# GpSimd's four multiplications of y by the last norm's row wait until the last column pair's sevens are folded

## The chip, the core and the metric

The kernel runs on one core of one Trainium2 chip. The metric is the device time of one execution in microseconds (us). The core has five engines that run their own instruction streams side by side: TensorE (PE, matrix products, with its weight loads listed apart as PEld), VectorE (DVE), ScalarE (ACT), GpSimd (POOL) and SyncE (SP, which here issues the DMA transfers). They meet only at semaphores: an instruction waits until another engine or a transfer has counted a semaphore up.

## The reference, cut to what matters

One decoder layer on 256 rows of 2048 columns: a token mixer (two groups of attention heads), then a channel mixer, each with a norm before and after. The change lies in the channel mixer's end, which is

```python
def rmsnorm(x, g):
    y = xf * lax.rsqrt(jnp.mean(xf * xf, axis=-1, keepdims=True) + EPS)
    return (y * g.astype(jnp.float32)).astype(x.dtype)
...
h = rmsnorm(x, pre_ffn_g[l])
u = causal_dwconv(h @ w_up[l], conv_w[l], conv_b[l])
gate, val = jnp.split(u, 2, axis=-1)
y = (jax.nn.gelu(gate, approximate=True) * val) @ w_down[l]
x = x + rmsnorm(y, post_ffn_g[l])
```

w_down has 5632 rows and 2048 columns, in float32. The last line divides y by its root mean square over the 2048 columns, multiplies by the row post_ffn_g and adds x.

## The kernel before

All products run on TensorE in a split form: a float32 weight tile `raw` that a DMA has brought is rounded by ACT into a high part (`whi`, L118 or L287), and DVE subtracts to get the rest (`wlo`, L121 or L288: `wlo = raw - whi`, two inputs in SBUF). A product is then three matmuls: high by high, high by low, low by high. There are five buffers for `raw`, five for `whi`, five for `wlo`. SP issues the load of a unit of 512 KB when DVE's subtraction has freed a `raw` buffer.

The channel mixer's 5632 inner columns are done in two halves of 22 blocks of 128. In each half, first the up-projections fill G (22 tiles of 128 x 512, high and low), then the down-projection adds its products to y, kept in `y_sb` (128 x 2 x 2048: two row blocks t, four column blocks n of 512). The down-projection goes over column pairs, `for n in (0, 2)`. Within a pair, some of the eleven steps u are done by `seven` (a 2 x 2 block product with seven products instead of eight; its four extra sums lie in the PSUM banks a, c, d, f and its combined weight tiles are made by DVE at L998 to L1001) and the rest by `four`, four plain products of the banks. The PSUM banks of seven's extra sums are brought into `y_sb` by `fold`: an ACT copy (L1035) and eight DVE operations, L1036 to L1043, of which the last one writes y22, columns 1536 to 2047 of row block 1, when n is 2.

When a column block is complete, `down` adds its bank to `y_sb` (DVE, L965), squares and sums it on ACT (L967), and, in the second half, multiplies it by the norm's row `gbf` on GpSimd (L969), in place. For the second half's first pair (n = 0, so the columns 0 to 1023 of both row blocks) these four multiplications, 128 x 512 each, are not issued at once: `later_on` collects their arguments in `gains`, and the loop issues them later, in the second pair's step i = 2 (`i == max((0, *at))`, where `at` is (0, 2)), on the lines just behind that pair's `fold`. They stand behind the fold in the program's text only: nothing that they read or write is touched by the fold.

DVE's, ACT's, GpSimd's and SP's order is made by a scheduler from the program's dependencies; TensorE's is the order of the text. At the very end (from L1128) all orders are that of the text. After the loop, TensorE finishes the last column block: for row block 0 with full 512-wide matmuls (L975, bank e), for row block 1 with two halves of 256 columns (L284, banks b1). Some units of that part are kept in `rest`. Then come `rstd_y` (a power on GpSimd, L1093), `finish` (L1104, DVE: y times the root plus x) and the output transfers.

The places that the steps below touch:

- L965, L967, L969: `down`; L1036 to L1043: `fold`; L1064 to L1066: the issue of the four multiplications.
- L121 and L288: DVE's subtraction for a weight unit, for `four` and `seven`. TensorE's matmuls with `wlo` wait for it.
- L1072: ACT's two copies of y (row block 1, columns 1536 to 2047) into the banks b1.
- L89 to L93: `w_parts` places `wlo` within its buffer at an offset of 14 x 4 or 4 x 4 elements, by the unit's turn; L49: `ROOM`, an unused tile of 112 columns in the pool `small`.

Memory is handed out pool by pool, one behind the other: `const`, `main`, `wp`, `small`, and behind `small` the pools `mixp` (with oT), `att`, `hold` and `ffn` (with G), which are opened later.

Of the kernel before, what the change touches and what calls it, by code (L numbers as in the profile page):

```python
# [8 lines left out]
F32 = mybir.dt.float32  # L9
# [3 lines left out]
ALU = mybir.AluOpType  # L13
# [4 lines left out]
P = 128  # L18
# [15 lines left out]
def hybrid_layer(ctx: ExitStack, tc: tile.TileContext, x, pre_mix_g, w_in, b_forget, sinks,  # L34
# [3 lines left out]
    pe, act, dve, pool, sp = nc.tensor, nc.scalar, nc.vector, nc.gpsimd, nc.sync  # L38
# [7 lines left out]
    small = ctx.enter_context(tc.tile_pool(name="small", bufs=4))  # L46
# [5 lines left out]
    def bank(tag="acc"):  # L52
        return ps.tile([P, 512], F32, tag=tag, bufs=4, name="bank_" + tag)
# [236 lines left out]
    with tc.tile_pool(name="mixp", bufs=1) as mp:  # L290
# [311 lines left out]
        for p0, npair, cols in ((0, 3, 384), (3, 3, 384), (6, 2, 272)):  # L602
# [13 lines left out]
            for t, b in enumerate(b2):  # L616
# [5 lines left out]
                if cols == 272:  # L622
                    dve.scalar_tensor_tensor(z[:, t, :], b[:, 256:272], rpre[t], bfb,
                                             op0=ALU.mult, op1=ALU.add)
# [195 lines left out]
    with tc.tile_pool(name="ffn", bufs=1) as fp:  # L820
# [27 lines left out]
        y_sb = main.tile([P, 2, D], F32, tag="y", name="y_sb")  # L848
# [59 lines left out]
        for half in range(2):  # L908
# [52 lines left out]
            gains = []  # L961

            def down(t, n, b, gain=None):
                ys = y_sb[:, t, n * 512:(n + 1) * 512]
                dve.tensor_tensor(ys, b, ys, op=ALU.add)  # L965
                if half:
                    act.activation(junk, ys, AF.Square, scale=D ** -0.5,  # L967
                                   accum_out=ysq[t][:, n:n + 1])
                    (gain or pool.tensor_tensor)(ys, ys, gbf[:, n * 512:(n + 1) * 512], op=ALU.mult)  # L969
# [17 lines left out]
            def seven(n, u, last, banks, opened):  # L987

                b, e, g, a, c, d, f = banks
                k = half * FHALF + u * 2  # L990
                top, low = [w_load(w_rows(w_down, k + i, 1, n * 512, 1024), 1, 1024)[0]
                            for i in range(2)]
                b11, b12, b21, b22 = (x[:, i:i + 512] for x in (top, low) for i in (0, 512))
                s1, s2, s3, s4 = [(sums[:, u, i * P:i * P + P],
                                   sums[:, u, 512 + i * P:640 + i * P]) for i in range(4)]
                (w11,) = split_into(w_parts(UNIT, held=False), top, 1)
                w21, w22 = split_into(w_parts(UNIT, held=False), low, 2)
                dve.tensor_tensor(b11, b12, b11, op=ALU.subtract)  # L998
                dve.tensor_tensor(b12, b22, b12, op=ALU.subtract)
                dve.tensor_tensor(b22, b22, b11, op=ALU.subtract)  # L1000
                dve.tensor_tensor(b21, b21, b22, op=ALU.subtract)  # L1001
                products(a, parts_of(u * 2, 0), *w11, opened, last)
                products(b, parts_of(u * 2 + 1, 0), *w21, opened)
                products(e, s4, *w22, opened)

                def others():
                    t1, t3 = split_into(w_parts(UNIT, held=False), top, 2)
                    t4, t2 = split_into(w_parts(UNIT, held=False), low, 2)
                    products(d, s1, *t1, opened, last)
                    products(f, s3, *t3, opened, last)  # L1010
                    products(c, s2, *t2, opened, last)
                    products(g, parts_of(u * 2 + 1, 1), *t4, opened)

                return others

            def four(n, u, pair, opened):
                hi, lo = w_unit(w_rows(w_down, half * FHALF + u * 2, 2, n * 512, 512), 2, 512)
                for i in range(2):
                    for t in range(2):
                        products(pair[t], parts_of(u * 2 + i, t), hi[:, i, :], lo[:, i, :], opened,  # L1020
                                 u == FHALF // 2 - 1 and i == 1)

            def fold(n, a, c, d, f):

                y11, y12, y21, y22 = (y_sb[:, t, m * 512:(m + 1) * 512] for t in range(2)
                                      for m in (n, n + 1))
                if half == 0:
                    act.copy(y11, a)
                    dve.tensor_tensor(y22, c, y11, op=ALU.add)
                    dve.tensor_tensor(y12, d, y22, op=ALU.add)  # L1030
                    dve.tensor_tensor(y21, f, y22, op=ALU.add)
                    dve.tensor_tensor(y22, d, y21, op=ALU.add)
                else:
                    s = fp.tile([P, 512], F32, tag="s", name="s")
                    act.copy(s, a)  # L1035
                    dve.tensor_tensor(y11, a, y11, op=ALU.add)  # L1036
                    dve.tensor_tensor(s, c, s, op=ALU.add)
                    dve.tensor_tensor(y12, y12, s, op=ALU.add)
                    dve.tensor_tensor(y12, d, y12, op=ALU.add)
                    dve.tensor_tensor(s, f, s, op=ALU.add)  # L1040
                    dve.tensor_tensor(y21, y21, s, op=ALU.add)
                    dve.tensor_tensor(s, d, s, op=ALU.add)
                    dve.tensor_tensor(y22, y22, s, op=ALU.add)  # L1043

            for n in (0, 2):
                opened = []
                tail = half and n
                at = SEVENS[half][n // 2]
                shared = [bank("att") for _ in range(4 if at else 0)]
                b, e, g = [bank() for _ in range(3)]  # L1050
                h = None if tail else bank()
                for i in range(FHALF // 2 - len(at)):
                    others = None
                    if i in at:
                        u = at.index(i)
                        others = seven(n, u, u == len(at) - 1, (b, e, g, *shared), opened)
                    four(n, len(at) + i, (b, g), opened)
                    if not tail:
                        four(n + 1, len(at) + i, (e, h), opened)
                    if others:  # L1060
                        others()
                    if at and i == at[-1]:
                        fold(n, *shared)
                    if i == max((0, *at)):  # L1064
                        for args, kw in gains:
                            pool.tensor_tensor(*args, **kw)  # L1066
                    if tail and i == (at[-1] + 4 if at else 0):
                        b1 = [bank("att"), bank("att")]
                        for x, cs in zip(b1, halves):
                            pe.matmul(x[:, cs], G[0][:, 0:P], G[0][:, 0:256], start=True,  # L1070
                                      stop=False)
                            act.copy(x[:, cs], y_sb[:, 1, 1536:2048][:, cs])  # L1072
                later_on = None if tail else lambda *args, **kw: gains.append((args, kw))
                for t, x in enumerate((b, g)):
                    down(t, n, x, later_on)
                if not tail:
                    for t, x in enumerate((e, h)):
                        down(t, n + 1, x, later_on)
# [30 lines left out]
        for u in range(len(at), FHALF // 2):  # L1109
# [4 lines left out]
            for i in range(2):  # L1114
                k = u * 2 + i
                args = k, hi[:, i, :], lo[:, i, :]
# [61 lines left out]
```

## Time and profile before

| what | value |
|---|---|
| time, median of 3 runs | 1058.31 us (1058.13 to 1058.46) |
| the profiled execution's own time | 1058.56 us |
| its span, first instruction to last | 1056.8 us |
| TensorE busy | 1046.5 us (99%), 5920 matmuls |
| VectorE busy | 820.8 us (78%) |
| ScalarE busy | 635.5 us (60%) |
| GpSimd busy | 259.0 us (25%) |
| granted TensorE clock | 0.998 of full speed |
| DMA, mean over the span | 195 GB/s read from HBM and written |

How to read it: the profile takes one execution, with each instruction's start and duration. The page sums the busy time by engine and by line, and follows the chain of work that ended last back from the end. The views of the trace quoted below give single instructions: start in us from the span's start, duration in us, engine, line, operation, what is written and read, and in brackets how long the engine stood idle before it and for whom. "xN" joins N neighbours of one kind. Matmuls overlap, so a matmul of 512 columns is listed with 0.39 us while the next one starts 0.227 us after it: the spacing of starts is what counts.

### The profile page before, as it was taken

What the parts mean: (1) busy time and instruction counts of PE and PEld (TensorE: products, weight loads), DVE (VectorE), ACT (ScalarE), POOL (GpSimd) and SP (SyncE); (2) the same over time, 40 slices, a digit from 0 to 9 for tenths busy, and PEclk for the clock granted to TensorE, in tenths of its full rate; (3) what the DMA queues carried; (4) which work ended last, traced back from release to release, by engine and by line L of the source; (5) the groups of instructions that cost most, each with busy time, mean ns of one, the idle gap of its engine ahead of it and who ended that gap; (6) DMA issues with size and microseconds to landing.
All of it is one profiled execution on the core that took longest, in us unless ns stands there. A gap on an engine that the chain in (4) does not pass through costs nothing.

```text
span 1056.8 us, 16351 instructions
## 1 busy us (share of the span) xinstructions
PE 1046.5 (99%) x5920; PEld 910.4 (86%) x5920; DVE 820.8 (78%) x1324; ACT 635.5 (60%) x1094; POOL 259.0 (25%) x282
## 2 busy tenths in 40 slices
PE   9999999999999999999999999999999999999996
PEld 7889988888889888888888888888888888888786
DVE  5989877886468787777768888867787777788983
ACT  7777757767557656656555555546566565655560
POOL 4253245431122433311112000003432221200301
PEclk9999999999999999999999999999999999999999
DMA  8645666655875766666665566766656665647483
GB/s 291 194 124 180 181 191 202 175 153 161 298 237 186 220 202 196 201 186 199 193 199 149 188 221 204 235 198 192 187 179 210 192 198 186 192 149 233 156 274 126
DMA packets 161965, 207.09 MB, mean 196 GB/s; under 512 B 6844, under 2 KB 131036, under 8 KB 160860
## 3 DMA queue, kind: packets, MB, share of 16 engines
q1 hardware_dynamic: 161564, 205.65, 62.0%
q8 instruction: 46, 0.75, 0.3%
q10 hardware_dynamic: 320, 0.40, 0.1%
q14 instruction: 35, 0.29, 0.1%
HBM read 201.68 MB, written 4.21 MB: 195 GB/s over the span
## 4 chain that ended last, share of the span: by engine, by line
PE 89%; DVE 4%; DMA 2%; issue 2%; ACT 1%; POOL 0%; SPq 0%; DVEq 0%; POOLq 0%; ACTq 0%
PE bank_acc L262 21%; PE bank_att L262 15%; PE bank_acc L284 13%; PE bank_acc L975 12%; PE bank_acc L269 11%; PE bank_att L269 7%; PE bank_att L975 2%; DMA raw<-in_w_down_dram 2%; DVE wlo L121 1%; PE bank_att L450 1%; PE bank_att L485 1%; PE bank_att L494 1%; DVE wlo L288 1%; PE bank_acc L881 1%; PE bank_acc L225 1%
## 5 line engine op out<-in xcount | busy, mean ns | idle before, releaser
L121 DVE TENSOR_TENSOR wlo<-raw,whi 128x1024 fp32r<-128x1024 f32 (+3 forms) x329 | 400.6, 1231 | 121.5 <-ACT whi L118 114.3
L118 ACT CAST whi<-raw 128x1024 fp32r<-128x1024 f32 (+3 forms) x328 | 333.5, 1033 | 174.6 <-issue 84.5
L262 PE MATMUL bank_acc<-hT,whi 128*128 128x512 f32 x1024 | 245.5, 392 | 0.0
L262 PEld LDWEIGHTS bank_acc<-hT,whi 128*128 128x128 f32 x1024 | 188.2, 188 | 37.1
L857 POOL TENSOR_TENSOR u<-u,rowf 128x256 f32<-128x256 f32 x88 | 95.6, 1107 | 440.1 <-DVE u L856 437.2
L262 PE MATMUL bank_att<-hT,whi 128*128 128x512 f32 x704 | 165.7, 390 | 0.0
L975 PE MATMUL bank_acc<-whi,G 128*128 128x512 f32 x492 | 159.5, 389 | 0.0
L262 PEld LDWEIGHTS bank_att<-hT,whi 128*128 128x128 f32 x704 | 130.6, 188 | 26.2
L269 PEld LDWEIGHTS bank_acc<-hT,wlo 128*128 128x128 f32 x1024 | 123.5, 188 | 3.2
L269 PE MATMUL bank_acc<-hT,wlo 128*128 128x256 f32 x1024 | 125.8, 278 | 0.0
L975 PEld LDWEIGHTS bank_acc<-whi,G 128*128 128x128 f32 x492 | 92.4, 188 | 19.0
L975 PE MATMUL bank_acc<-wlo,G 128*128 128x512 f32 x246 | 95.9, 390 | 0.4 <-DVE wlo L121 0.4
L269 PEld LDWEIGHTS bank_att<-hT,wlo 128*128 128x128 f32 x704 | 83.6, 188 | 1.9
L269 PE MATMUL bank_att<-hT,wlo 128*128 128x256 f32 x704 | 84.0, 277 | 0.0
L284 PE MATMUL bank_acc<-whi,oT 128*128 128x512 f32 (+1 forms) x272 | 81.8, 379 | 0.0
L287 ACT CAST whi<-raw 128x1024 fp32r<-128x1024 f32 (+1 forms) x56 | 51.7, 942 | 35.2 <-PE bank_acc L975 15.9
L288 DVE TENSOR_TENSOR wlo<-raw,whi 128x1024 fp32r<-128x1024 f32 (+1 forms) x56 | 62.2, 1133 | 6.5 <-ACT whi L287 6.5
L284 PEld LDWEIGHTS bank_acc<-whi,oT 128*128 128x128 f32 x272 | 50.2, 188 | 9.3
L975 PEld LDWEIGHTS bank_acc<-wlo,G 128*128 128x128 f32 x246 | 46.2, 188 | 10.2 <-DVE wlo L121 0.8
L284 PE MATMUL bank_acc<-wlo,oT 128*128 128x512 f32 (+1 forms) x136 | 51.2, 377 | 0.0
L859 ACT ACTIVATE yg<-u,cw 128x256 f32<-128x256 f32 x44 | 26.5, 602 | 37.2 <-POOL u L857 37.2
L284 PE MATMUL bank_acc<-whi,hT 128*128 128x384 f32 (+1 forms) x192 | 46.9, 323 | 0.0
(250 smaller groups left out, 1317.7 us busy)
## 6 DMA issues: line engine op xcount, KB each, us to landing
raw<-in_w_up_dram SPq DMA_DIRECT2D x176, 512.0 KB, 4.5
raw<-in_w_down_dram SPq DMA_DIRECT2D x88, 512.0 KB, 4.9
raw<-in_w_in_dram SPq DMA_DIRECT2D x51, 512.0 KB, 5.0
raw<-in_w_out_dram SPq DMA_DIRECT2D x32, 512.0 KB, 4.6
raw<-in_w_in_dram SPq DMA_DIRECT2D x16, 384.0 KB, 3.3
cb<-c_dram SPq DMA_DIRECT2D x8, 256.0 KB, 4.5
x_sb<-in_x_dram SPq DMA_DIRECT2D x2, 1024.0 KB, 6.0
x_dram<-x_sb SPq DMA_DIRECT2D x2, 1024.0 KB, 5.8
```

The costliest lines, as they stand in the source:

```text
L118: i1 = act.copy(hi[:, cs], raw[:, cs])
L121: i2 = dve.tensor_tensor(lo[:, cs], raw[:, cs], hi[:, cs].bitcast(F32), op=ALU.subtract)
L225: pe.matmul(b, hi[:, a, m * P:(m + 1) * P], hT[:, kt, 0:512], start=(kt == 0), stop=(kt == KT - 1))
L262: pe.matmul(b, hi[:, a, m * P:(m + 1) * P], hT[:, kt, 0:512], start=(kt == 0), stop=(last == (0, kt)))
L269: pe.matmul(b[:, 256:512], lo[:, a, m * P:(m + 1) * P], hT[:, u * 4 + a, 0:256], start=False, stop=(last == (1, u * 4 + a)))
L284: pe.matmul(b, a, r[:, cols], start=(first and i == 0), stop=(last and i == 2))
L287: act.copy(hi, src)
L288: dve.tensor_tensor(lo, src, hi.bitcast(F32), op=ALU.subtract)
L450: pe.matmul(sb[e][:, cs], a[r, t * P:(t + 1) * P], b[r, 0:nk], start=(n == 0), stop=(n == 2))
L857: pool.tensor_tensor(u[:, 2:258], u[:, 2:258], rowf, op=ALU.mult)
L859: act.activation(y, u[:, 2:258], AF.Identity, bias=cw[:, 3, ch:ch + 1], scale=cw[:, 2, ch:ch + 1])
L975: pe.matmul(b, x, r, start=b not in opened and not i, stop=closes and i == 2)
```

## The change

```diff
                     if i == max((0, *at)):
+                        if gains:
+                            past = small.tile([P, 1], F32, tag="past", bufs=1, name="past")
+                            tc.keep_in_program_order(
+                                pool.tensor_scalar(past, y_sb[:, 1, 1536:1537], 1.0, None,
+                                                   op0=ALU.mult))
                         for args, kw in gains:
-                            pool.tensor_tensor(*args, **kw)
+                            tc.keep_in_program_order(pool.tensor_tensor(*args, **kw))
```

A small GpSimd operation, `past`, is put ahead of the four multiplications. It reads one column of y22, the block that `fold` writes last (L1043), so it cannot start before the fold has ended; the four are held behind it in GpSimd's order. `past` itself is used by nobody.

GpSimd's stream at this place, as a difference (minus: before, plus: changed; `y_sb` is y, `gbc_ffn` the norm's row, `u` the convolution's input):

```order
 L857 TENSOR_TENSOR u_3946<-u_3946,rowf 128x256
 L857 TENSOR_TENSOR u_3947<-u_3947,rowf 128x256
-L1066 TENSOR_TENSOR y_sb<-y_sb,gbc_ffn 128x512 x4
+L1068 TENSOR_SCALAR past<-y_sb 128x1
+L1071 TENSOR_TENSOR y_sb<-y_sb,gbc_ffn 128x512 x4
 L969 TENSOR_TENSOR y_sb<-y_sb,gbc_ffn 128x512 x3
```

The stream has one instruction more, ahead of the four; the four keep their place between the last convolution's `u` and the last three multiplications. Their time moves, since `past` waits for VectorE.

VectorE's stream at the fold, the same before and in the changed kernel (the instruction that `past` waits for is L1043; `wlo` and `rest` are low parts of weight units):

```order
L121 TENSOR_TENSOR wlo<-raw,whi 128x1024
L1038 TENSOR_TENSOR y_sb<-y_sb,s 128x512
L121 TENSOR_TENSOR wlo<-raw,whi 128x1024
L1039 TENSOR_TENSOR y_sb<-bank_att,y_sb 128x512
L1040 TENSOR_TENSOR s<-bank_att,s 128x512
L121 TENSOR_TENSOR wlo<-raw,whi 128x1024
L1041 TENSOR_TENSOR y_sb<-y_sb,s 128x512
L1042 TENSOR_TENSOR s<-bank_att,s 128x512
L121 TENSOR_TENSOR wlo<-raw,whi 128x1024
L1043 TENSOR_TENSOR y_sb<-y_sb,s 128x512
L121 TENSOR_TENSOR rest<-raw,rest 128x1024
L121 TENSOR_TENSOR wlo<-raw,whi 128x1024
```

No instruction of VectorE, ScalarE, TensorE or SyncE moves. In the built program the tile `past` takes 32 bytes of each partition at the end of the pool `small`, and every tile of the pools behind it, oT and G among them, lies 32 bytes further on than before.

## The prediction

> **What bounds the kernel now.** First the page:
>
> ```profile
> span 1056.8 us, 16351 instructions
> PE 1046.5 (99%) x5920; PEld 910.4 (86%) x5920; DVE 820.8 (78%) x1324; ACT 635.5 (60%) x1094; POOL 259.0 (25%) x282
> PE 89%; DVE 4%; DMA 2%; issue 2%; ACT 1%; POOL 0%; SPq 0%; DVEq 0%; POOLq 0%; ACTq 0%
> ```
>
> TensorE is the bound: it is busy 99% and holds 89% of the chain that ended last. GpSimd is on that chain with 0%. So the four multiplications can only matter through what they do to TensorE's supply. The chain in order of time, at the place where they run (about 987 to 997 us), shows VectorE in it twice:
>
> ```profile
> 993.75 2.32 DVE wlo L121
> ...
> 1004.34 1.22 DVE wlo L288
> ...
> 1006.34 11.56 PE bank_acc L975 x51
> ```
>
> Before and after this stretch the chain is TensorE alone. The timeline of GpSimd and VectorE says why (the third row is the same multiplication form elsewhere, with the minimum, median and maximum in ns):
>
> ```profile
> L1066 POOL TENSOR_TENSOR y_sb<-y_sb,gbc_ffn x4: 2265/2473/2977, 987.2 to 994.9; 128x512 f32<-128x512 f32 x4
> 987.16 10.05 POOL L1066 TENSOR_TENSOR y_sb<-y_sb,gbc_ffn 128x512 f32<-128x512 f32 x4 [53.07 <-ACT junk L967]
> L709 POOL TENSOR_TENSOR mix_sb<-mix_sb,gbc_mix x9: 743/1291/1744, 299.6 to 333.0; 128x512 f32<-128x512 f32 x7, 128x256 f32<-128x256 f32 x2
> ```
>
> ```profile
> 979.70 0.69 DVE L288 TENSOR_TENSOR wlo<-raw,whi 128x512 fp32r<-128x512 f32 x1
> 987.43 1.22 DVE L121 TENSOR_TENSOR wlo<-raw,whi 128x1024 fp32r<-128x1024 f32 x1
> 988.57 1.28 DVE L965 TENSOR_TENSOR y_sb<-bank_acc,y_sb 128x512 f32<-128x512 f32 x2
> ...
> 991.80 2.03 DVE L288 TENSOR_TENSOR wlo<-raw,whi 128x1024 fp32r<-128x1024 f32 x1 [0.21 <-ACT whi L287]
> 993.75 2.31 DVE L121 TENSOR_TENSOR wlo<-raw,whi 128x1024 fp32r<-128x1024 f32 x1
> 995.99 2.91 DVE L288 TENSOR_TENSOR wlo<-raw,whi 128x512 fp32r<-128x512 f32 x2
> ```
>
> A multiplication that takes 1.29 us at the median of L709 takes 2.27 to 2.98 us here. Meanwhile VectorE's subtractions, 1.22 us for 1024 columns and 0.69 us for 512, take 2.03, 2.31 and (a pair, 0.69 + 1.22 less the 0.09 by which neighbours overlap, so 1.82) 2.91 us. They take turns: each multiplication makes one subtraction wait, and VectorE loses 0.81 + 1.09 + 1.09 = **2.99 us**. The two L965 additions, which have one input in PSUM, lose nothing in the same ten microseconds.
>
> **What TensorE loses to that.** TensorE's starts around the two places:
>
> ```profile
> 995.09 0.61 PE L975 MATMUL bank_acc<-whi,G 128*128 128x512 f32 x2
> 996.12 0.50 PE L975 MATMUL bank_acc<-wlo,G 128*128 128x512 f32 x1 [0.42 <-DVE wlo L121]
> 996.45 0.63 PE L975 MATMUL bank_acc<-whi,G 128*128 128x512 f32 x2
> ...
> 1003.52 0.39 PE L975 MATMUL bank_att<-whi,sums 128*128 128x512 f32 x1
> 1003.88 0.50 PE L975 MATMUL bank_att<-wlo,sums 128*128 128x512 f32 x1
> 1004.21 0.63 PE L975 MATMUL bank_att<-whi,sums 128*128 128x512 f32 x2
> ...
> 1004.91 0.63 PE L975 MATMUL bank_att<-whi,sums 128*128 128x512 f32 x2
> 1005.61 0.50 PE L975 MATMUL bank_att<-wlo,sums 128*128 128x512 f32 x1
> 1005.94 0.40 PE L975 MATMUL bank_att<-whi,sums 128*128 128x512 f32 x1
> ```
>
> At full pace 512-column matmuls start 0.227 us apart (11.56 us / 51, from the chain). The first place: 995.09 to 996.12 is 1.03 where two need 0.45, and the next step is 0.33: lost 0.58 + 0.10 = 0.68. The second: 0.36, 0.33, 0.70 (for two) and 0.33 where 0.227, 0.227, 0.454 and 0.227 would do: 0.13 + 0.10 + 0.25 + 0.10 = 0.58. Together **1.26 us**. Each time TensorE goes on just after a VectorE subtraction ends (993.75 + 2.31 = 996.06; 1004.34 + 1.21 = 1005.55).
>
> **The change part by part.** *Removed at 987 to 997 us:* the four multiplications. VectorE then runs 991.80 to 998.8 in 2.99 us less. At the first place the subtraction that TensorE waits for ends near 994.2 instead of 996.06, and TensorE wants it at 995.55: 1.3 us to spare. For the second place the path goes over ACT:
>
> ```profile
> 995.58 1.05 ACT L118 CAST whi<-raw 128x1024 fp32r<-128x1024 f32 x1 [1.39 <-PE bank_acc L975]
> 1001.34 1.05 ACT L287 CAST whi<-raw 128x1024 fp32r<-128x1024 f32 x1 [4.71 <-DVE raw L999]
> ```
>
> The rounding at 1001.34 waits for VectorE's L999, which stands in VectorE's order behind the subtraction for the unit rounded at 995.58, a time set by TensorE and not by the contention. So that subtraction can begin at 996.65 instead of 999.42, all that follows comes 2.75 us earlier, and the two that TensorE waited for end near 1001.1 and 1002.8. TensorE, then 0.68 us earlier, wants them at 1003.1 and 1004.8: 2 us to spare. Both losses go: -1.26 us. Behind them TensorE has no gap, so nothing more can be had there.
>
> *Added:* `past`, one column. No such instruction is in the trace; GpSimd's power of one column takes 0.55 us with its start (below), so I bound it by 0 and 0.55 and take 0: nobody reads it, and what it can hold up is VectorE once.
>
> *Moved:* the four multiplications behind L1043, before at 1018.44 + 0.69 = 1019.1, and near 1016.5 if VectorE's 2.75 us carry through. They can again cost VectorE one turn each, 4 x 1.09 = 4.4 us (below it, 0: where VectorE idles, they cost nothing). What is late then? Rows of three of VectorE's subtractions behind the fold, of TensorE's first use of each, behind its first matmul into b1, and of ACT's copies:
>
> ```profile
> 1018.44 0.69 DVE L1043 TENSOR_TENSOR y_sb<-y_sb,s 128x512 f32<-128x512 f32 x1
> ...
> 1020.75 1.22 DVE L121 TENSOR_TENSOR wlo<-raw,whi 128x1024 fp32r<-128x1024 f32 x1
> ...
> 1023.03 1.22 DVE L121 TENSOR_TENSOR wlo<-raw,whi 128x1024 fp32r<-128x1024 f32 x1
> ...
> 1031.14 2.08 DVE L121 TENSOR_TENSOR wlo<-raw,whi 128x1024 fp32r<-128x1024 f32 x1 [0.16 <-ACT whi L118]
> ```
>
> ```profile
> 1024.12 0.28 PE L284 MATMUL bank_att<-whi,G 128*128 128x256 f32 x1
> ...
> 1026.47 0.40 PE L975 MATMUL bank_acc<-wlo,G 128*128 128x512 f32 x1
> ...
> 1029.29 0.40 PE L975 MATMUL bank_acc<-wlo,G 128*128 128x512 f32 x1
> ...
> 1038.92 0.39 PE L975 MATMUL bank_acc<-wlo,G 128*128 128x512 f32 x1
> ```
>
> ```profile
> 1022.56 0.67 ACT L1072 COPY bank_att<-y_sb 128x256 f32<-128x256 f32 x2
> ```
>
> The unit subtracted at 1020.75 is ready at 1021.97 and used at 1026.47: 4.5 us of lead. That at 1023.03 is ready at 1024.25, used at 1029.29: 5.0 us. The last is ready at 1033.22, used at 1038.92: 5.7 us. Two turns stand before the first (2.2 us), four before the second (4.4 us, with `past` 4.9). TensorE comes 1.26 us sooner, VectorE up to 2.75 us sooner; even with no such advance only the second would be late, by 4.9 - (5.0 - 1.26) = 1.2 us. I take 0, for the advance is more than that. ACT's copies end at 1023.23 and TensorE needs them at 1024.12, now at 1022.86; they stand behind roundings that wait for loads that VectorE's earlier subtractions set off, before the fold's end, so they move forward too. If they did not, 0.4 us of the gain would go. GpSimd's own queue behind the four:
>
> ```profile
> 1028.10 4.03 POOL L969 TENSOR_TENSOR y_sb<-y_sb,gbc_ffn 128x512 f32<-128x512 f32 x2 [30.89 <-ACT junk L967]
> ...
> 1049.63 0.55 POOL L1093 TENSOR_TENSOR ry<-rv,mhalf 128x1 f32<-128x1 f32 x1 [5.99 <-DVE rv L1091]
> ```
>
> With 16.5 + 0.55 + 10.05 (as long as now) the four end near 1027.1; the two L969 then start within a microsecond of now and have until 1041, so the end, from TensorE's last matmul on, stays as it is.
>
> *The address.* The new tile moves oT and G by 32 bytes. They are TensorE's stationary operand in 1152 matmuls of 512 columns and in 158 of 256 or fewer. A stationary operand at such a place is there already: the first `wlo` of a projection lies 14 x 4 elements, 224 bytes, into its buffer, the others 64 bytes. The widest difference in pace between alike matmuls that I find is this, 32 of 256 columns each:
>
> ```profile
> 331.47 4.00 PE L881 MATMUL bank_acc<-hT,whi 128*128 128x256 f32 x32
> 568.49 3.81 PE L269 MATMUL bank_acc<-hT,wlo 128*128 128x256 f32 x32
> L269 PEld LDWEIGHTS bank_acc<-hT,wlo 128*128 128x128 f32 x1024 | 123.5, 188 | 3.2
> ```
>
> The slow row has its weights at their buffer's start, the fast one at 64 and 224 bytes: 0.19 us / 32 = 6 ns each, in favour of the odd place if anything. For the 158 narrow ones (many now at the slow pace) that bounds a gain of 158 x 6 ns = 0.95 us. With 512 columns weights load in 188 ns inside a step of 227, so I take 0; the bound on the other side is in the third rival.
>
> **The sum.** 1058.56 (this execution: span 1056.8 and 1.76 around it) - 1.26 + 0 + 0 = 1057.30. This execution lies 0.25 over the median of 1058.31, so the forecast for a median is **1057.05 us**, 0.12% down: within the 0.2% (2.1 us) that a measurement of this kernel can tell from no change.
>
> **Rivals.** *The loss only moves.* The 2.99 us come from VectorE and GpSimd taking turns, and the fold's end is followed by more subtractions, so the turns come again; TensorE pays where a lead is used up. Price 1.2 us for the one late unit above, time 1058.25. For it: in each of the rows behind the fold VectorE is at a subtraction of 1.2 us, as it was at 991. Against: leads of 4.5 us and more, where at 996 there were none. The Trainium skill, page "SBUF — State Buffer", section "SBUF: two separate sides", states such a rule: VectorE with two SBUF inputs and GpSimd share one port pair as an exclusive lock, and the loser is blocked for the whole instruction. This case's trace agrees (2.31 against 1.22 us, and L965 with its PSUM input not slowed); by that rule the price stays wherever VectorE has such work waiting, which speaks against this change and is why this rival has the second largest chance.
>
> *Nothing changes.* If the fold ended before the four could have begun, `past` would hold nothing. The trace has 32 us between 987.16 and 1019.1, so this is nearly excluded; or GpSimd's turns are not what delays VectorE. Time 1058.3.
>
> *Slower, by the address.* If the 6 ns carried over to the 512-column matmuls with G and oT: 1152 x 6 ns = 6.9 us, less 1.26: 1064 us. It decides from 3 ns per matmul on (1152 x 2.9 ns = 3.4 us, which is 1.26 + 2.1). Against it: 188 ns for a load at either place, hidden below 227.
>
> *More than the sum.* If narrow matmuls and attention (its tiles move too) gain at the new places: up to 0.95 us and somewhat more, 1056 us.
>
> **How the numbers follow.** Forecast 0.67 (by itself 1056.1 to 1057.7). The loss moves 0.13, nothing changes 0.05, slower by the address 0.09, more than the sum 0.06. The range leaves out the address case and part of the last: 1056.0 to 1058.6. Faster by over 0.2% (below 1056.2): the last case and a little of the first, 0.08. Slower (over 1060.4): the address case and a little of the second, 0.10. The same: 0.82.
>
> **What would show it.** In the profile after: the four near 1017 to 1027 us; VectorE's subtractions between 991 and 999 at 1.2 us; TensorE without a step over 0.24 us between 995 and 1006; subtractions of about 2.3 us behind the fold, and still no gap of TensorE between 1010 and 1047. Wrong would be: gaps at 1023 to 1030 (the loss moved), gaps left at 1004 (another wait beneath), or 512-column steps in the down-projection that are no longer 0.227 us (the address).

## The result, and the profile after

The changed kernel takes **1064.59 us** (median of 6 runs, 1064.45 to 1065.06) against 1058.22 us before (6 runs, 1057.73 to 1058.83): a ratio of 1.0061, 95% interval 1.0051 to 1.0071. It is 6.4 us slower, where 1.2 us faster was forecast.

The page of the changed kernel: span, busy time, share of the last chain.

```profile
span 1062.9 us, 16352 instructions
PE 1052.9 (99%) x5920; PEld 910.6 (86%) x5920; DVE 822.6 (77%) x1324; ACT 635.9 (60%) x1094; POOL 258.0 (24%) x283
PE 96%; DVE 1%; issue 1%; DMA 1%; ACT 0%; SPq 0%; POOL 0%; DVEq 0%; POOLq 0%; ACTq 0%
```

TensorE's share of the chain went up from 89% to 96%, VectorE's went from 4% to 1%. TensorE's own starts say the same: between 985 and 1055 us six of its steps took more than 0.245 us before, and none does in the changed kernel. So the waits for VectorE did go, and TensorE itself became slower. First the part that was meant, GpSimd's and VectorE's timelines of the changed kernel:

```profile
1021.45 0.24 POOL L1068 TENSOR_SCALAR past<-y_sb 128x1 f32<-128x1 f32 x1 [82.26 <-DVE y_sb L1043]
1021.65 8.01 POOL L1071 TENSOR_TENSOR y_sb<-y_sb,gbc_ffn 128x512 f32<-128x512 f32 x4
```

```profile
997.55 1.23 DVE L288 TENSOR_TENSOR wlo<-raw,whi 128x1024 fp32r<-128x1024 f32 x1 [0.22 <-ACT whi L287]
998.69 1.22 DVE L121 TENSOR_TENSOR wlo<-raw,whi 128x1024 fp32r<-128x1024 f32 x1
999.83 1.92 DVE L288 TENSOR_TENSOR wlo<-raw,whi 128x512 fp32r<-128x512 f32 x2
...
1020.67 0.68 DVE L1043 TENSOR_TENSOR y_sb<-y_sb,s 128x512 f32<-128x512 f32 x1
1022.00 2.04 DVE L121 TENSOR_TENSOR rest<-raw,rest 128x1024 fp32r<-128x1024 f32 x1 [0.64 <-ACT rest L118]
1023.96 2.31 DVE L121 TENSOR_TENSOR wlo<-raw,whi 128x1024 fp32r<-128x1024 f32 x1
1026.19 2.31 DVE L121 TENSOR_TENSOR rest<-raw,rest 128x1024 fp32r<-128x1024 f32 x1
1028.43 3.45 DVE L121 TENSOR_TENSOR wlo<-raw,whi 128x1024 fp32r<-128x1024 f32 x2
```

The three entries that took 2.03, 2.31 and 2.91 us before are back to 1.23, 1.22 and 1.92. The four multiplications run behind the fold, and there each costs VectorE a turn again: 2.04, 2.31, 2.31 and 3.45 (for two) instead of 1.22 each. Now the chain of the changed kernel at places where only TensorE is in it:

```profile
273.19 53.13 PE bank_acc L284 x228
...
1011.88 11.89 PE bank_acc L975 x51
```

The same pieces of the chain before:

```profile
272.28 51.86 PE bank_acc L284 x228
...
1006.34 11.56 PE bank_acc L975 x51
```

The same 228 and 51 matmuls take longer: 53.13 / 228 = 0.2330 us a step (from one start to the next) against 51.86 / 228 = 0.2275, and 11.89 / 51 = 0.2331 against 11.56 / 51 = 0.2267. The first piece is the output projection of the token mixer, some 700 us ahead of the first instruction that the change moves. The groups of the page show which matmuls (columns: count, busy us, mean ns, idle), changed kernel first, then before:

```profile
L262 PE MATMUL bank_acc<-hT,whi 128*128 128x512 f32 x1024 | 245.6, 392 | 0.0
L975 PE MATMUL bank_acc<-whi,G 128*128 128x512 f32 x492 | 162.6, 395 | 0.0
L284 PE MATMUL bank_acc<-whi,oT 128*128 128x512 f32 (+1 forms) x272 | 83.1, 384 | 0.0
```

```profile
L262 PE MATMUL bank_acc<-hT,whi 128*128 128x512 f32 x1024 | 245.5, 392 | 0.0
L975 PE MATMUL bank_acc<-whi,G 128*128 128x512 f32 x492 | 159.5, 389 | 0.0
L284 PE MATMUL bank_acc<-whi,oT 128*128 128x512 f32 (+1 forms) x272 | 81.8, 379 | 0.0
```

Matmuls whose stationary operand is G or oT, tiles that the new tile has pushed 32 bytes on, are 5 to 6 ns longer. L262, whose operands did not move, is the same.

### The profile page after: what moved, and what is told of

It is laid out like the page before. It is cut to its first block, busy times and chain, and to the rows that moved or that the text cites. A ratio compares the mean times of both kernels' runs of the same rounds, so it can differ in the third digit from the quotient of the medians.

```text
span 1062.9 us, 16352 instructions
## 1 busy us (share of the span) xinstructions
PE 1052.9 (99%) x5920; PEld 910.6 (86%) x5920; DVE 822.6 (77%) x1324; ACT 635.9 (60%) x1094; POOL 258.0 (24%) x283
## 4 chain that ended last, share of the span: by engine, by line
PE 96%; DVE 1%; issue 1%; DMA 1%; ACT 0%; SPq 0%; POOL 0%; DVEq 0%; POOLq 0%; ACTq 0%
PE bank_acc L262 21%; PE bank_acc L975 17%; PE bank_att L262 15%; PE bank_acc L284 13%; PE bank_acc L269 11%; PE bank_att L269 8%; PE bank_att L975 4%; PE bank_att L450 1%; PE bank_att L485 1%; PE bank_att L494 1%; PE bank_acc L881 1%; PE bank_acc L225 1%; DMA x_in<-in_x_dram 1%; PE bank_att L225 1%; PE bank_att L496 0%
## 5 line engine op out<-in xcount | busy, mean ns | idle before, releaser
L262 PE MATMUL bank_acc<-hT,whi 128*128 128x512 f32 x1024 | 245.6, 392 | 0.0
L262 PEld LDWEIGHTS bank_acc<-hT,whi 128*128 128x128 f32 x1024 | 188.2, 188 | 37.1
L262 PE MATMUL bank_att<-hT,whi 128*128 128x512 f32 x704 | 165.7, 390 | 0.0
L975 PE MATMUL bank_acc<-whi,G 128*128 128x512 f32 x492 | 162.6, 395 | 0.0
L262 PEld LDWEIGHTS bank_att<-hT,whi 128*128 128x128 f32 x704 | 130.6, 188 | 26.3
L975 PEld LDWEIGHTS bank_acc<-whi,G 128*128 128x128 f32 x492 | 92.4, 188 | 21.9
L975 PE MATMUL bank_acc<-wlo,G 128*128 128x512 f32 x246 | 97.2, 395 | 0.0
L975 PEld LDWEIGHTS bank_acc<-wlo,G 128*128 128x128 f32 x246 | 46.2, 188 | 10.9
```

The source lines that it names most:

```text
L262: pe.matmul(b, hi[:, a, m * P:(m + 1) * P], hT[:, kt, 0:512], start=(kt == 0), stop=(last == (0, kt)))
L975: pe.matmul(b, x, r, start=b not in opened and not i, stop=closes and i == 2)
```

## The experiments

Two questions: is it the 32 bytes or the multiplications' new place, and if the bytes, what about them? Times are medians; "before" is the kernel before, run on the same chip beside each.

| run | what | us | ratio to before (95%) |
|---|---|---|---|
| e1 | changed kernel, places put back | 1057.14 | 0.9988 (0.998 to 0.9997) |
| e2 | kernel before, oT and G and behind +32 bytes | 1064.52 | 1.0057 (1.0043 to 1.0071) |
| e3 | kernel before, all but the constants +32 bytes | 1058.20 | 0.9999 (0.9989 to 1.0008) |
| e4 | changed kernel, G put back to +512, oT at +32 | 1059.10 | 1.0009 (1.0 to 1.0018) |
| e5 | kernel before, +64 bytes | 1064.98 | 1.0061 (1.0047 to 1.0075) |
| e6 | kernel before without the four | 1057.23 | 0.9991 (0.9981 to 1.0) |
| e7 | kernel before, +128 bytes | 1064.43 | 1.0059 (1.0039 to 1.0079) |
| e8 | kernel before, +512 bytes | 1058.16 | 0.9999 (0.9989 to 1.001) |
| e9 | kernel before, +256 bytes | 1058.29 | 1.0 (0.9989 to 1.0011) |

**e1: the changed kernel with the old places.**

```diff
-ROOM = 112
+ROOM = 104
```

> The changed kernel, with the unused tile in the pool small 32 bytes smaller, so that oT, G and all behind them lie where they lay before. Theory 1 (the 32 bytes of the new tile cost TensorE 5 to 6 ns in each 512-column matmul with G or oT, the wait itself gains 1.26 us): 1057.0 us, 1.2 us under the kernel before; no TensorE step over 0.24 us between 995 and 1006 us, and 0.227 us steps throughout the down-projection. Rival (the four multiplications in their new place cost the time): 1064.6 us as in the changed kernel.

Measured 1057.14 us. Its chain and GpSimd's timeline:

```profile
1004.91 11.56 PE bank_acc L975 x51
...
1016.70 6.15 PE bank_acc L975 x27
```

```profile
1015.53 0.24 POOL L1068 TENSOR_SCALAR past<-y_sb 128x1 f32<-128x1 f32 x1 [81.53 <-DVE y_sb L1043]
1015.74 8.01 POOL L1071 TENSOR_TENSOR y_sb<-y_sb,gbc_ffn 128x512 f32<-128x512 f32 x4
```

The steps are 0.2267 us again (11.56 / 51), no step of TensorE between 985 and 1055 us is over 0.245 us, and the four stand behind the fold as in the changed kernel. The multiplications' new place is therefore not what costs the time; with the old places the change is worth 1.0 us (1058.16 - 1057.14). This is also the version that beats both kernels, if only by 0.12%.

**e2: the 32 bytes alone.**

```diff
-ROOM = 112
+ROOM = 120
```

> The kernel before, with the unused tile 32 bytes larger: oT, G and all behind them move by 32 bytes, and nothing else is changed. Theory 1: slower by 5.0 us (792 matmuls with G) plus 2.0 us (360 with oT), so near 1065.2 us, more than the changed kernel, since the 1.26 us of waits are still in it. Rival (the moved multiplications are the cause): 1058.2 us.

Measured 1064.52 us, with the four at their old place. The 32 bytes alone cost 6.4 us. It came 0.7 us lower than expected, and TensorE's timeline of this run says why: of the gaps that VectorE's lost turns cause, one small one is left, 0.56 us for two steps at 1010.32 and 0.33 at 1010.88:

```profile
1010.32 0.61 PE L975 MATMUL bank_att<-whi,sums 128*128 128x512 f32 x2
1010.88 0.50 PE L975 MATMUL bank_att<-wlo,sums 128*128 128x512 f32 x1
1011.21 0.40 PE L975 MATMUL bank_att<-whi,sums 128*128 128x512 f32 x1
```

VectorE still loses its turns in this run (2.03, 2.32 and 2.91 us for the same three entries), but TensorE, slower by 2.8% in these steps, comes later to each `wlo`. So beside the slower pace, holding back the four was worth nothing: 1064.59 us with them behind the fold, 1064.52 with them at the old place.

**e3: both operands moved.** An unused tile in the first pool made larger, so that weights, G, oT and the rest move together.

```diff
-    const.tile([P, 112], F32, tag="room", name="room")
+    const.tile([P, 120], F32, tag="room", name="room")
```

> The kernel before, with the unused tile of the pool const 32 bytes larger: everything but the constants moves by 32 bytes, stationary and moving operands alike. If it is the difference between the two operands' places that counts: 1058.2 us, and 0.227 us steps everywhere. If a stationary operand that does not start at a multiple of 64 bytes is slow by itself: 1152 matmuls as in the changed kernel and some 1800 of the projections, 5.5 ns each, 16 us more: 1074 us.

Measured 1058.20 us, no difference. Its chain:

```profile
272.31 51.85 PE bank_acc L284 x228
...
1005.83 11.57 PE bank_acc L975 x51
```

oT and G lie where they lay in e2, but so do `whi` and `wlo`, the moving operands, by the same 32 bytes, and the pace is the old one. So it is not the stationary operand's own place that counts, but its distance from something that stayed in e2 and moved in e3. The moving operand is one such tile, but others moved in e3 too. The changed kernel's own trace tells them apart. In 24 of oT's 360 matmuls of 512 columns the moving tiles `whi` and `wlo` lie in the pool `hold`, which stands behind `small` and moved by the same 32 bytes. By the built program's addresses oT lies a multiple of 512 bytes from the moving operand in these 24, and 32 bytes past such a multiple in the other 336. The 24 run from 309.5 to 315.0 us:

```profile
308.59 0.63 PE L284 MATMUL bank_acc<-whi,oT 128*128 128x512 f32 x2
309.06 0.40 PE L284 MATMUL bank_acc<-wlo,oT 128*128 128x512 f32 x1
309.29 0.63 PE L284 MATMUL bank_acc<-whi,oT 128*128 128x512 f32 x2
...
310.66 0.62 PE L284 MATMUL bank_acc<-whi,oT 128*128 128x512 f32 x2
311.12 0.39 PE L284 MATMUL bank_acc<-wlo,oT 128*128 128x512 f32 x1
311.34 0.62 PE L284 MATMUL bank_acc<-whi,oT 128*128 128x512 f32 x2
...
316.14 0.63 PE L284 MATMUL bank_acc<-whi,oT 128*128 128x512 f32 x2
316.60 0.40 PE L284 MATMUL bank_acc<-wlo,oT 128*128 128x512 f32 x1
316.84 0.63 PE L284 MATMUL bank_acc<-whi,oT 128*128 128x512 f32 x2
```

Three steps take 0.70 us ahead of the 24 and behind them, and 0.68 us, the old pace, within them. For these matmuls it is therefore the **distance between the two operands' places** that counts.

**e5, e7, e9, e8: how large a distance.** The kernel before with ROOM larger by 16, 32, 64 and 128 columns: 64, 128, 256 and 512 bytes.

```diff
-ROOM = 112
+ROOM = 128
```

> The kernel before, with the unused tile 64 bytes larger: oT, G and all behind them move by 64 bytes. If only the place within 64 bytes counts: 1058.2 us. If a larger unit counts (512 bytes, one row of a weight tile): near 1065 us as with 32 bytes.

> The kernel before, with oT, G and all behind them moved by 128 bytes. If the unit is 128 bytes: 1058.2 us and steps of 0.227 us. If it is larger: 1064.5 to 1065 us and steps of 0.233 us, as with 32 and 64 bytes.

> The kernel before, with oT, G and all behind them moved by 256 bytes. If the unit is 512 bytes: 1064.5 to 1065 us and steps of 0.233 us, as with 32, 64 and 128 bytes. If it is 256 bytes: 1058.2 us.

> The kernel before, with oT, G and all behind them moved by 512 bytes. If the unit is 512 bytes or a part of it: 1058.2 us. If any distance costs: 1064.5 to 1065 us.

64 and 128 bytes cost as much as 32 (1064.98 and 1064.43 us), 256 and 512 bytes nothing (1058.29 and 1058.16 us). My guess after e5, a unit of 512 bytes, was wrong by half: of the distances tried, multiples of 256 bytes are free and the others are not, for the matmuls with oT and G. The same 51 matmuls in the chain of these four runs, in the order of 64, 128, 256 and 512 bytes, each from its own trace:

```profile
1012.28 11.90 PE bank_acc L975 x51
```

```profile
1011.69 11.85 PE bank_acc L975 x51
```

```profile
1006.15 11.58 PE bank_acc L975 x51
```

```profile
1005.85 11.59 PE bank_acc L975 x51
```

**e4: G put back, oT not.** The changed kernel with an unused tile of 480 bytes ahead of G.

```diff
     with tc.tile_pool(name="ffn", bufs=1) as fp:
+        fp.tile([P, 120], F32, tag="pad", name="pad")
```

> The changed kernel, with an unused tile of 480 bytes at the start of the pool ffn, so that G lies 512 bytes from where it lay before, while oT stays 32 bytes off. Theory (the distance between the places of the two operands, counted in units of 512 bytes, costs each 512-column matmul with G or oT about 6 ns): only the 360 with oT still pay, 2.0 us, and the 1.26 us of the waits are gained again, since the down-projection is back at its pace: 1057.1 + 2.0 = 1059.1 us. If 512 bytes are not the unit: 1064.6 us as in the changed kernel.

Measured 1059.10 us, as expected. The two pieces of its chain (L976 is what was L975):

```profile
272.73 53.13 PE bank_acc L284 x228
```

```profile
1006.68 11.56 PE bank_acc L976 x51
```

Slow with oT, at full pace with G. This splits the loss: 1059.10 - 1057.14 = 2.0 us is oT's (336 x 6.0 ns by the steps of e1 and of the changed kernel; the 24 with tiles in `hold` pay nothing), and 1064.59 - 1059.10 = 5.5 us is G's (792 x 6.4 ns = 5.1 us by the steps). Attention's tiles are moved in this run too; oT's 2.0 us leave nothing for them.

**e6: without the four multiplications.**

```diff
                         for args, kw in gains:
-                            pool.tensor_tensor(*args, **kw)
+                            pass
```

> The kernel before without the four multiplications (the columns 0 to 1023 of the result lack the norm's row). If their turns with VectorE at 987 to 997 us cause TensorE's waits and cost nothing behind the fold: 1057.1 us, as with the addresses put back. If the four still cost something in their new place: less than 1057.1 us. If TensorE's waits have another cause: 1058.2 us.

Measured 1057.23 us, the same as e1 within the interval. This kernel leaves the norm's row out of the columns 0 to 1023, so it only prices the four. They cost TensorE about 1 us at their old place and nothing that can be seen behind the fold.

## Why the prediction was wrong, point by point

- **The step that failed** is the address term of the sum: "With 512 columns weights load in 188 ns inside a step of 227, so I take 0". It measured 792 x 6.4 ns = 5.1 us with G and 336 x 6.0 ns = 2.0 us with oT, 7.1 us in all. (Of the 1152 matmuls counted there, the 24 with moving tiles in `hold` keep their distance and pay nothing.) The weight loads are still listed at 188 ns; that they fit inside the step did not protect it. The rows that the prediction leaned on were narrow matmuls, 256 columns, where weights at odd places ran faster. Its argument that such places are there already holds for the projections' `wlo`, used 256 columns wide; in the output projection and the down-projection `wlo` starts at its buffer's start. Of the 512-column matmuls in the trace of before, nearly all have their operands a multiple of 512 bytes apart. The exceptions are 40 of attention's value products (L494), 128 bytes short of such a multiple: 23 of their steps took 234 to 238 ns and 15 took 224 to 230 (the other two are longer by a wait), a hint, though not a clean one, that the prediction did not use.
- **The third rival** was the right account: it named the step that would be longer and the matmuls, with 6 ns each, 6.9 us and 1064 us; measured were 6.0 to 6.4 ns and 1064.59 us. That the 6 ns fit so well is luck: they came from narrow matmuls, where the odd place was the faster one. What was wrong was the rival's chance of 0.09, and a range that left it out. For the 512-column case nothing but an argument stood against it.
- **The waits' 1.26 us** are nearly right by themselves: e1, which has the forecast's condition (no change of places), measured 1057.14 against 1057.05 forecast, 1.0 us under the kernel before, and TensorE's two places of waiting are gone there. In the changed kernel they are gone as well, but the slower pace does nearly all of that by itself: with the four at their old place only 0.21 us of them was left (e2). The held-back multiplications and the slower pace remove the same gaps, so beside the slower pace the change gains nothing.
- **The moved cost** was right in size and in effect. VectorE loses 0.82 + 1.09 + 1.09 + 1.09 = 4.1 us behind the fold in the changed kernel (4.4 forecast as the most), `past` takes 0.24 us (0 to 0.55), and TensorE waits for none of it. In e1 the four run from 1015.7 to 1023.8 (16.5 to 27.1 forecast). The rival "the loss only moves" is refuted for the time, though not for VectorE: the turns move, as the lock rule of the Trainium skill (page "SBUF — State Buffer", section "SBUF: two separate sides") has it, but the leads cover them.
- **Still open:** the parts add up to 7.1 - 1.26 = 5.8 us against 6.4 measured. Beside e1, which has the changed kernel's order at the old places, the gap is smaller: 1064.59 - 1057.14 = 7.45 us against 7.1. Of this rest, 0.25 us lies in the 168 steps with the operand `sums`, which stand among those with G: 226.7 ns on average in e1, 228.2 in the changed kernel, though neither of their operands moved. So the distance of a matmul's own operands is not the whole account. Nor do the runs show why the distance counts: the trace lists no wait in these steps, only a longer spacing.

## What to carry to other kernels

A new tile, however small, moves every pool behind it: compare the addresses of the built program before and after any edit that allocates, and take the bytes out of an unused tile so that the operands of long matmul runs keep their distance. Test an edit's idea apart from what its bookkeeping does; here one constant separated +6.4 us from -1.0 us. When a thousand instructions will meet a new condition, search the trace for instructions of the same form that meet it already; where it has none, the bound is the estimate to plan with, and its chance is not small.

## What the runs showed of the hardware that was not expected

- A 512-column float32r matmul with oT or G that follows its own weight load starts 0.227 us after its neighbour when the places of its two operands differ by a multiple of 256 bytes (0, 256 and 512 tried), and 0.232 to 0.233 us after it at 32, 64 and 128 bytes. Both operands moved by 32 bytes give 0.2269 us (e3, and the 24 in the changed kernel's own trace).
- Smaller groups do not follow this rule alone. With G 128 bytes off (e7), the 112 matmuls with `sums` that read `whi` take a median step of 232 ns against 227, at unmoved operands. The eight value products with `ph` and `vpa` are listed with 397 ns before and 393 in the changed kernel, though their two operands moved together. No run shows the reason.
- For matmuls of 256 columns it is rather the other way: 32 with weights at a multiple of 512 bytes took 4.00 us, 32 with weights 64 and 224 bytes off 3.81 us (both rows in the prediction). The narrow ones with G, which moved along by 32 bytes, went from 119.4 to 118.3 ns a step with `whi` and from 119.1 to 117.4 ns with `wlo`, 0.1 us in all. No run here varied the distance for these alone.
- VectorE and GpSimd, both with two SBUF inputs and both waiting, take turns one by one: the four multiplications cost VectorE three turns at the old place (0.81, 1.09 and 1.09 us) and four behind the fold (0.82 and three times 1.09 us).
